# Convolution taps ordered behind the query and key operands, one pass for both key ranges, other tap rates: a two-layer trunk on one Trainium2 core

## The chip, the cores and the metric

The kernel runs on one core of a Trainium2 chip. The metric is the device time of one execution in microseconds; lower is better. The kernel before takes 1058.18 us, the median of 3 runs (1057.49 to 1059.27). One of its executions was also profiled, and every number on where time goes comes from that one.

## The reference

A trunk of two layers over 256 latent tokens (a grid of 4 rows by 64 columns) and 256 context tokens, all in fp32, model width 1024. The part of a layer that matters here:

```python
def conv_branch(p_glu, dw, dw_b, ln_g, ln_b, w_o):
    a, g = jnp.split(p_glu, 2, axis=-1)
    u = a * jax.nn.sigmoid(g)
    u = dwconv1d(u, dw, dw_b)              # depthwise, 31 taps, 512 channels
    u = jax.nn.silu(layernorm(u, ln_g, ln_b))
    return u @ w_o
...
    p = h @ w_in[l]                        # columns: conv | q | k | v | gates
    q = rope_2d(q, pos_row, pos_col)
    k = rope_2d(k, pos_row, pos_col)
    y_conv = conv_branch(p[..., :GLU_END], ...)
    y_attn = merge_heads(neighbourhood_attention(q, k, v, k_c, v_c, na_rpb[l])) @ w_na_out[l]
    x = x + g1 * gated_merge(p[..., QKV_END:], y_conv, y_attn, w_out[l])
```

`neighbourhood_attention` has 8 heads of 64. Each query sees a clamped window of 4 rows by 16 columns, with a bias per relative position, and all 256 context keys, under one softmax. In layer 0 the context tokens run through the same weights (512 columns in all) and attend to each other; in layer 1 only keys and values of the context are needed. A gated MLP with a width-3 convolution follows in each layer.

## The kernel before

**Products.** Activations lie transposed: 128 channels on the partitions, tokens along the free axis. Each fp32 product is three fp32r products on TensorE (PE): high times high (L197), high times low of the activation (L198), low of the weight times high (L199). A weight block of 128x1024 arrives by DMA, ScalarE (ACT) casts its high part (L167), VectorE (DVE) subtracts to get the low part (L168). For some blocks ACT makes both (L216, L217) and a DMA of POOL adds the raw weight. One `group` is 24 products into one PSUM bank.

**Side work.** Generators are stepped once at each slot, which a group calls at its end, and a group of 512 columns also in its middle. The generators are: the taps of the depthwise convolution (`conv_run`), the attention (`Attention.run`, which issues scores, softmax, transposes and values in steps), the modulation products of the next norms on VectorE (L304), and the norms.

**Taps.** The convolution is 4 channel blocks (`cb[0]` to `cb[3]`) by 31 taps per layer, on VectorE. The first of a block is L671, the others L673: `cb = u * w + cb`, over 128x512 elements in layer 0 and 128x256 in layer 1. `rate` says how many taps a slot issues. `conv_tap` orders a tap behind the instruction that the list `after` holds; that list is filled by the attention alone, with the latest softmax minimum (`scores`, L516: adds the bias and takes the extreme of a row) or maximum (`ctx_scores`, L530). This is an order on VectorE's own queue. After the last tap VectorE adds the four blocks (L949 to L951; the first two on POOL in layer 1), and TensorE sums that over the channels for the LayerNorm (L955).

**Queries and keys.** `qk(j)` handles two heads, j = 0 to 3 ("pair j" below): a group for Q and one for K, then the rotary embedding on VectorE (L859 multiply, L860 shuffle, L861 multiply, L864 or L869 add), then a high part by ACT (L881) and a low part by VectorE (L882). K's latent columns are stored twice, in two ranges of 40 columns by 4 rows (128x160), one for each half of the queries; so K takes an ACT and a VectorE pass for each range and, for its context columns, one more of each that reads the PSUM bank directly.

**Attention.** Scores (TensorE, L495) go to four PSUM tiles (`sc` twice, `pt`, `main`); L516 on VectorE, exponential on ACT (L519), reciprocal on VectorE (L521), scaling on ACT (L522), transposes on TensorE (L561), copies of the transposes out of PSUM on ACT (L564), then values (L578). The context's own softmax has L530, L535, L537, L540 and L567 in these places. It is done for two pairs at a time, so twice in layer 0.

The instructions are put in order on each engine by a scheduler from the program's dependencies, its code order and the `issue_after` hints. Where the PSUM banks and buffers go is decided with it.

## Time and profile before

| what | us |
| --- | --- |
| median of 3 runs | 1058.18 |
| profiled execution | 1054.58 |
| its span, first to last instruction | 1052.8 |
| TensorE busy | 1032.4 (98%) |
| VectorE busy | 893.2 (85%) |
| ScalarE busy | 565.6 (54%) |
| 120 taps of 128x512, layer 0 | 89.1 |
| 120 taps of 128x256, layer 1 | 55.7 |
| mean granted TensorE clock, share of full | 0.997 |

TensorE's busy time is nearly the span, so what is left to read is each stretch in which it waits. A row of the waits says which engine and line waited for which, for how long in total, how often and how long at most. A row of a timeline has the start, the length, the engine, the line, the operation, what it writes and reads, and in brackets the idle time ahead of it and what ended that. The lengths of two rows that follow each other can overlap by a little, since the next instruction starts before the one ahead has written its last result.

### The profile page before, as it was taken

The page shows a single profiled execution, that of the slowest core. Times are in us where ns is not written, and L with a number is a line of the kernel's source. Part 1 is how long each engine was busy: PE and PEld are TensorE (multiplying, and loading weights), DVE is VectorE, ACT ScalarE, POOL GpSimd, SP SyncE. Part 2 cuts the span into 40 slices and gives each one's busy share as a digit, 9 for nine tenths or more (in the row PEclk, how much of TensorE's full clock was granted, in tenths as well). Part 3 has the DMA queues.
Part 4 walks back from the last instruction along what each step waited for, and adds up shares of the span by engine and source line. Part 5 has one row for each costly group of instructions (what it writes and reads, how often), then busy time and mean ns, then how long its engine had stood idle before and what let it go on. Part 6 is the DMA issues. An engine that isn't in the chain of part 4 may idle for free.

```text
span 1052.8 us, 17991 instructions
## 1 busy us (share of the span) xinstructions
PE 1032.4 (98%) x6886; PEld 932.9 (89%) x6886; DVE 893.2 (85%) x1608; ACT 565.6 (54%) x921; POOL 43.7 (4%) x59
## 2 busy tenths in 40 slices
PE   9999999999999999999999999999999999999997
PEld 7787788888889988888888889999889999999996
DVE  6568899999998787878788888799899988988883
ACT  4458768545434644444444223545777666766652
POOL 1111110011000000000000000000000000000000
PEclk9999999999999999999999999999999999999998
DMA  9989674888945345454545887556734485666781
GB/s 374 305 221 229 156 181 121 258 255 236 305 146 177 104 140 160 140 164 143 166 145 160 301 289 249 180 189 209 208 123 135 161 292 176 193 201 199 221 283 57
DMA packets 59511, 209.26 MB, mean 199 GB/s; under 512 B 7201, under 2 KB 7457, under 8 KB 59425
## 3 DMA queue, kind: packets, MB, share of 16 engines
q1 hardware_dynamic: 54384, 190.77, 55.3%
q0 software_dynamic: 4752, 17.30, 8.7%
q8 instruction: 54, 0.88, 0.3%
q14 instruction: 33, 0.26, 0.1%
q10 hardware_dynamic: 288, 0.04, 0.0%
HBM read 187.63 MB, written 1.05 MB: 179 GB/s over the span
## 4 chain that ended last, share of the span: by engine, by line
PE 68%; DVE 17%; ACT 5%; DMA 4%; issue 3%; SPq 1%; DVEq 0%; ACTq 0%
PE main L197 20%; PE main L198 20%; PE main L199 20%; DVE cb L673 6%; PE main L736 4%; DVE wlo L168 3%; DMA raw<-in_wall 2%; DVE t L304 2%; DMA own<-in_wada 1%; SPq L728 1%; PE sc L197 1%; PE sc L199 1%; PE sc L198 1%; DVE qk L882 1%; ACT pp L519 1%
## 5 line engine op out<-in xcount | busy, mean ns | idle before, releaser
L197 PE MATMUL main<-h,whi 128*128 128x256 f32 (+1 forms) x1328 | 433.1, 326 | 1.2 <-DVE qk L882 1.2
L198 PE MATMUL main<-h,whi 128*128 128x256 f32 (+1 forms) x1328 | 430.2, 324 | 0.9 <-DVE h L1001 0.7
L199 PE MATMUL main<-h,wlo 128*128 128x256 f32 (+1 forms) x1328 | 429.9, 324 | 1.2 <-DVE wlo L168 1.1
L167 ACT CAST whi<-raw 128x1024 fp32r<-128x1024 f32 (+1 forms) x211 | 218.3, 1039 | 234.8 <-PE main L198 173.6
L168 DVE TENSOR_TENSOR wlo<-raw,whi 128x1024 fp32r<-128x1024 f32 (+1 forms) x211 | 253.6, 1208 | 67.2 <-ACT whi L167 66.4
L197 PEld LDWEIGHTS main<-h,whi 128*128 128x128 f32 x1328 | 252.8, 190 | 22.0 <-issue 1.3
L199 PEld LDWEIGHTS main<-h,wlo 128*128 128x128 f32 x1328 | 252.5, 190 | 18.5 <-DVE wlo L168 1.8
L198 PEld LDWEIGHTS main<-h,whi 128*128 128x128 f32 x1328 | 252.7, 190 | 18.3 <-DVE h L1001 1.0
L304 DVE CUSTOM_DVE_ANT_0 t<-own,sb,par 128x1024 bf16<-128x1024 f32 x120 | 151.8, 1282 | 6.8 <-DMA own<-in_wada 6.8
L673 DVE SCALAR_TENSOR_TENSOR cb<-u,par,cb 128x512 f32<-128x512 f32 (+1 forms) x240 | 144.7, 620 | 2.8
L198 PE MATMUL main<-fl,whi 128*128 128x256 f32 (+1 forms) x396 | 122.8, 310 | 0.0
L197 PE MATMUL main<-fh,whi 128*128 128x256 f32 (+1 forms) x396 | 122.8, 310 | 0.0
L199 PE MATMUL main<-fh,wlo 128*128 128x256 f32 (+1 forms) x396 | 122.5, 310 | 0.0
L197 PEld LDWEIGHTS main<-fh,whi 128*128 128x128 f32 x396 | 75.6, 191 | 3.8 <-ACT fh L1095 0.2
L198 PEld LDWEIGHTS main<-fl,whi 128*128 128x128 f32 x396 | 75.6, 191 | 3.7 <-DVE fl L1096 0.2
L199 PEld LDWEIGHTS main<-fh,wlo 128*128 128x128 f32 x396 | 75.5, 191 | 3.6
L216 ACT CAST whi<-raw 128x1024 fp32r<-128x1024 f32 x33 | 34.6, 1049 | 36.0 <-PE main L198 30.5
L404 ACT ACTIVATE h<-t,mod 128x256 fp32r<-128x256 f32 x56 | 25.2, 503 | 34.8 <-DVE t L403 34.3
L218 POOL DMA_DIRECT2D wlo<-raw x33 | 28.9, 877 | 258.9 <-ACT wlo L217 107.6
L736 PE MATMUL main<-whi,h 128*128 128x512 f32 x128 | 38.5, 386 | 0.2
L1105 ACT ACTIVATE t<-t 128x512 f32<-128x512 f32 x22 | 13.9, 632 | 41.3 <-DVE t L1074 41.3
L217 ACT ACTIVATE wlo<-whi 128x1024 fp32r<-128x1024 f32 x33 | 35.0, 1061 | 0.5
(214 smaller groups left out, 1268.8 us busy)
## 6 DMA issues: line engine op xcount, KB each, us to landing
raw<-in_wall SPq DMA_DIRECT2D x240, 512.0 KB, 4.3
own<-in_wada SPq DMA_DIRECT2D x72, 512.0 KB, 4.7
wlo<-raw POOLq DMA_DIRECT2D x33, 512.0 KB, 5.4
raw<-in_wada SPq DMA_DIRECT2D x16, 512.0 KB, 5.8
bias<-in_bias_t SPq DMA_DIRECT2D x8, 520.0 KB, 5.3
row<-in_wada SPq DMA_DIRECT2D x8, 512.0 KB, 5.1
sb<-in_crow SPq DMA_DIRECT2D x5, 512.0 KB, 4.8
x<-in_xt SPq DMA_DIRECT2D x4, 512.0 KB, 5.1
```

The source lines that it names most:

```text
L167: act.copy(hi[:, c], r[:, c])
L168: dve.tensor_tensor(lo[:, c], r[:, c], hi[:, c].bitcast(F32), ALU.subtract)
L197: pe.matmul(ps, w[0], order(xh), start=start, stop=False)
L198: pe.matmul(ps, w[0], order(xl), start=False, stop=False)
L199: pe.matmul(ps, w[1], order(xh), start=False, stop=stop)
L216: act.copy(hi, r)
L217: act.mul(lo, hi.bitcast(F32), -1.0)
L218: pool.dma_start(lo, r, accum_op=ALU.add)
L304: dve.tensor_tensor_reduce(tmp().bitcast(BF16), r, v, 1.0, pr(l, BADA + n, 1), ALU.mult, ALU.add, mods[l][:, n, s : s + 1])
L404: high = act.activation(hi[:, c], y[:, c], AF.Identity, bias=b)
L673: dve.scalar_tensor_tensor(cb[j], src, w, cb[j], ALU.mult, ALU.add)
L736: mm = pe.matmul(pv[t], h1[n == 1][k][:, c], runs(w[n == 2][:, b]), start=k + n == 0, stop=k == KD - 1 and n == 2)
```

## The change

Line numbers in the changed kernel are 4 higher up to the taps (a tap is L677 there, a block's first L675), the rotary lines are L865 to L875, ACT's and VectorE's passes L884 and L885, the LayerNorm lines L958 to L967.

1. After each Q and each K operand, `after[0]` is set to the last low part of that operand. Taps that are issued from then on stand behind the whole chain on VectorE.
2. K's two latent ranges are written by one ACT copy (L889) and one VectorE subtraction (L890) over 128x2x4x40 elements. The two ranges are one access pattern with one more dimension, made by the helper `steps`. That is 8 ACT and 8 VectorE instructions less over the 8 K operands.
3. Rates: layer 0 starts at 3 taps a slot (before 2), has 1.5 in Q's and K's groups, and 4 after the first pair (before 3). Layer 1 keeps 3.

```diff
+    def steps(a, first, *dims):
+
+        return bass.AP(tensor=a.tensor, offset=a.offset + first, ap=[a.ap[0], *dims])
...
                 conv = conv_run()
-                rate[0] = 3 if last else 2.0
+                rate[0] = 3.0
                 add_side(conv)
 
                 def qk(j):
 
                     att.ahead(j - 2)
+                    if not last:
+                        rate[0] = 1.5
...
                         else:
-                            rv_ = r1[:, LAT].rearrange("p (r c) -> p r c", r=ROWS)
                             to = [([f[:, a, KCTX] for a in range(2)], ctx_)]
-                            for d, c in ((slice(0, KL), slice(GW - TC, GW)), (slice(KX, KN), slice(0, TC))):
-                                to.append(([f[:, a, d].rearrange("p (c r) -> p r c", r=ROWS) for a in range(2)], rv_[:, :, c]))
                         for (hi, lo), src in to:
                             act.activation(hi, src, AF.Identity, scale=sc)
                             end = dve.scalar_tensor_tensor(lo, src, sc, hi.bitcast(F32), ALU.mult, ALU.subtract)
+                        if what:
+                            hi, lo = (steps(f[:, a], 0, (KX, 2), (1, ROWS), (ROWS, TC)) for a in range(2))
+                            src = steps(r1, GW - TC, (TC - GW, 2), (GW, ROWS), (1, TC))
+                            act.copy(hi, src)
+                            end = dve.tensor_tensor(lo, src, hi.bitcast(F32), ALU.subtract)
+                        after[0] = end
                         both.append(f)
                     att.pair(j, *both, bt, end)
+                    rate[0] = 3.0 if last else 4.0
...
                     for j in range(1, 4):
                         glu_groups(j)
                         qk(j)
-                        rate[0] = 3
```

The rows below are instructions in the order in which an engine has them, without times: line, operation, what it writes and reads, the elements, and a count where a row stands for several. Numbers in names tell buffers apart.

VectorE in layer 0 at K of pair 1 (the scores of this pair are what the prediction calls place A). `main_943` and `main_946` are K's PSUM bank. Before:

```order
L859 TENSOR_TENSOR t_1012<-main_943,rope_196 128x256
L860 STREAM_SHUFFLE t_1013<-main_943 128x256
L673 SCALAR_TENSOR_TENSOR cb_0_184<-u_0_197,par,cb_0_184 128x512
L861 TENSOR_TENSOR t_1013<-t_1013,rope_196 128x256
L882 SCALAR_TENSOR_TENSOR qk_1018<-main_943,qk_1018 128x256
L869 TENSOR_TENSOR t_1012<-t_1012,t_1013 128x256
L673 SCALAR_TENSOR_TENSOR cb_0_184<-u_0_197,par,cb_0_184 128x512 x2
L882 SCALAR_TENSOR_TENSOR qk_1018<-t_1012,qk_1018 128x4x40 x2
L673 SCALAR_TENSOR_TENSOR cb_0_184<-u_0_197,par,cb_0_184 128x512 x3
L516 ISA sc_1063,mx_1079<-sc_1063,bias_893 128x2x208
```

The same engine and place in the changed kernel, from the last rotary addition on:

```order
L875 TENSOR_TENSOR t_1014<-t_1014,t_1015 128x256
L885 SCALAR_TENSOR_TENSOR qk_1020<-main_946,qk_1020 128x256
L890 TENSOR_TENSOR qk_1020<-t_1014,qk_1020 128x2x4x40
L677 SCALAR_TENSOR_TENSOR cb_0_184<-u_0_197,par,cb_0_184 128x512
L675 TENSOR_SCALAR cb_1_185<-u_1_198,par 128x512
L677 SCALAR_TENSOR_TENSOR cb_0_184<-u_0_197,par,cb_0_184 128x512
L677 SCALAR_TENSOR_TENSOR cb_1_185<-u_1_198,par,cb_1_185 128x512
L677 SCALAR_TENSOR_TENSOR cb_0_184<-u_0_197,par,cb_0_184 128x512
L677 SCALAR_TENSOR_TENSOR cb_1_185<-u_1_198,par,cb_1_185 128x512
L516 ISA sc_1065,mx_1081<-sc_1065,bias_897 128x2x208
L516 ISA mx_1081 128x1
L677 SCALAR_TENSOR_TENSOR cb_1_185<-u_1_198,par,cb_1_185 128x512
```

Three taps have left the inside of the chain, six stand between it and the first minimum instead of three, and the minima have a tap between them, where before none stood before the second.

VectorE ahead of the second context softmax of layer 0 (place C). Before:

```order
L673 SCALAR_TENSOR_TENSOR cb_2_186<-u_2_199,par,cb_2_186 128x512 x4
L168 TENSOR_TENSOR wlo_2160<-raw_2158,whi_2159 128x1024
L673 SCALAR_TENSOR_TENSOR cb_2_186<-u_2_199,par,cb_2_186 128x512 x5
L596 TENSOR_TENSOR ol_2_194<-po_1902,oh_2_190 128x4x4x16
L530 TENSOR_REDUCE mx_343_1945<-sc_1917 128x2
```

In the changed kernel:

```order
L677 SCALAR_TENSOR_TENSOR cb_2_186<-u_2_199,par,cb_2_186 128x512
L168 TENSOR_TENSOR wlo_2163<-raw_2161,whi_2162 128x1024
L677 SCALAR_TENSOR_TENSOR cb_2_186<-u_2_199,par,cb_2_186 128x512 x9
L959 TENSOR_TENSOR ss_2225<-ss_2225,cb_2_186 128x512
L596 TENSOR_TENSOR ol_2_194<-po_1900,oh_2_190 128x4x4x16
L530 TENSOR_REDUCE mx_343_1943<-sc_1915 128x2
```

Nine taps of one block and the second LayerNorm addition have taken the place of five taps. Behind the low parts of K of pairs 2 and 3 the changed order likewise has 8 taps of one block each, where 5 and 3 stood. On ACT, a cast of the next weights (L167), which stood ahead of the last two scalings (L540) of this softmax, stands behind them and behind a gate's activation (L715).

TensorE and VectorE at the LayerNorm sum of layer 0 (place D), where `ss` is the sum of the blocks, `po` what TensorE makes of it, and `main_2345` the group after it. TensorE in the changed kernel:

```order
L199 MATMUL main_2288<-h_175,wlo_2292 128x512
L964 MATMUL po_2326<-ss_2225,one 128x512
L197 MATMUL main_2345<-h_168,whi_2347 128x512
L198 MATMUL main_2345<-h_176,whi_2347 128x512
L199 MATMUL main_2345<-h_168,wlo_2348 128x512
```

VectorE there:

```order
L304 ISA t_2320,mod_105<-own_2245,sb_2146,par 128x1024
L304 ISA mod_105 128x1
L960 TENSOR_TENSOR ss_2225<-ss_2225,cb_3_187 128x512
L304 ISA t_2322,mod_105<-own_2245,sb_2149,par 128x1024
L304 ISA mod_105 128x1
L168 TENSOR_TENSOR wlo_2348<-raw_2346,whi_2347 128x1024
```

TensorE's L964 stands one group, 24 products, earlier in the program than L955 did, and the low part of the next group's weights (`wlo_2348`) stands behind the sum and a modulation product. From the first L530 of the second context softmax to L960, VectorE has 28 taps, 1 weight split, 5 modulation products (two rows each) and no other LayerNorm addition; before it had 33 taps and a block's first, 3 splits, 6 modulation products and one addition.

In layer 1 K's group of pair 3 gets another PSUM bank: before, the last reader of its bank was VectorE's pass over the context columns of pair 2's K (L882), now it is ACT's exponential of the last score tile of the softmax that runs then (L519). Ahead of that softmax's minima VectorE has a tap before each, and the shuffle and second multiply of the rotary chain behind them. TensorE's instructions are as many as before.

## The prediction

> **What bounds the kernel now.** I read the busy row of the page first, then TensorE's waits, then the groups of VectorE, then the timelines at each wait that the change could touch. The busy row:
>
> ```profile
> PE 1032.4 (98%) x6886; PEld 932.9 (89%) x6886; DVE 893.2 (85%) x1608; ACT 565.6 (54%) x921; POOL 43.7 (4%) x59
> ```
>
> TensorE (PE) has work in 1032.4 of 1052.8 us, and the change leaves its work alone. So VectorE (DVE) and ScalarE (ACT) count only where TensorE waits for them. The waits of TensorE that name an engine the change touches:
>
> ```profile
> PE sc L495 <- ACT pT L567: 1.7, 1, 1.7
> PE main L197 <- DVE qk L882: 1.2, 2, 0.6
> ...
> PE po L955 <- DVE ss L951: 1.0, 1, 1.0
> PE sc L495 <- ACT qk L881: 0.9, 1, 0.9
> PE sc L495 <- DVE qk L882: 0.6, 1, 0.6
> PE pt L561 <- ACT pp L522: 0.3, 1, 0.3
> ```
>
> The columns are the total, the number of waits and the longest, in us. What the view lists besides lies in norms, weight splits and the program's two ends. These six sum to 1.7 + 1.2 + 1.0 + 0.9 + 0.6 + 0.3 = 5.7 us: that is the ceiling, half a per cent of the time. VectorE in the stretches where most of these waits lie (columns: length, then busy time and count of PE, PEld, DVE, ACT, POOL, then clock, DMA share, GB/s):
>
> ```profile
> 90.00:130.00 40.00, 36.29 (x270) 30.01 (x271) 35.87 (x80) 32.32 (x72) 5.97 (x7) 1.00 0.71 168
> 130.00:180.00 50.00, 49.80 (x344) 41.51 (x342) 46.69 (x100) 37.03 (x84) 4.35 (x5) 1.00 0.64 156
> ```
>
> VectorE is busy 35.9 of 40 and 46.7 of 50 us, so a tap that leaves one place there comes back soon after. What the change can win is order, not work. The groups:
>
> ```profile
> L673 DVE SCALAR_TENSOR_TENSOR cb<-u,par,cb 128x512 f32<-128x512 f32 x120 | 89.1, 751 | 1.5
> L673 DVE SCALAR_TENSOR_TENSOR cb<-u,par,cb 128x256 f32<-128x256 f32 x120 | 55.7, 489 | 1.3
> L882 DVE SCALAR_TENSOR_TENSOR qk<-t,qk 128x160 fp32r<-128x160 f32 x16 | 7.8, 531 | 0.3
> ```
>
> **The price of a merged K copy.** Between the two tap rows 256 more elements cost 751 - 489 = 262 ns, so some 489 - 262 = 227 ns of an instruction do not depend on its length. By that estimate one pass over 320 elements takes 227 + 327 = 0.55 us, where two of 160 take 2 x (227 + 164) = 0.78 us (a row below shows two in 0.81). A merged pair saves about 0.25 us of VectorE. No row shows the four-dimensional pattern: at best it is as dense as estimated, at worst it runs at the 531 ns per 160 of the row above and saves nothing. I take 0.2. Eight pairs are 1.6 us of VectorE, but the path gets it only at the first place below. The Trainium skill, page "VectorE: DVE Perf Modes", section "The TRN2 errata — SBUF-src ops pay a fixed extra latency per instruction", speaks against a gain of this size: its table gives 58 cycles per VectorE instruction, thus 0.06 us at 0.96 GHz for a merged pair, and by it the first place gets 0.15 us less; the tap rows show 227 ns, nearer the longer term that the same section measures, and I go by the rows.
>
> **Place A, scores of pair 1, layer 0.** VectorE, then ACT, then PE:
>
> ```profile
> 92.40 0.42 DVE L859 TENSOR_TENSOR t<-main,rope 128x256 f32<-128x256 f32 x1
> ...
> 93.09 0.74 DVE L673 SCALAR_TENSOR_TENSOR cb<-u,par,cb 128x512 f32<-128x512 f32 x1
> 93.74 0.42 DVE L861 TENSOR_TENSOR t<-t,rope 128x256 f32<-128x256 f32 x1
> ...
> 94.74 1.54 DVE L673 SCALAR_TENSOR_TENSOR cb<-u,par,cb 128x512 f32<-128x512 f32 x2
> 96.20 0.81 DVE L882 SCALAR_TENSOR_TENSOR qk<-t,qk 128x160 fp32r<-128x160 f32 x2
> 96.91 2.33 DVE L673 SCALAR_TENSOR_TENSOR cb<-u,par,cb 128x512 f32<-128x512 f32 x3
> 99.16 0.59 DVE L516 CUSTOM_DVE_ANT_0 sc<-sc,bias 128x416 f32<-128x416 f32 x1
> ```
>
> ```profile
> 94.24 1.08 ACT L217 ACTIVATE wlo<-whi 128x1024 fp32r<-128x1024 f32 x1
> 95.20 0.79 ACT L881 ACTIVATE qk<-t 128x160 fp32r<-128x160 f32 x2
> ...
> 100.44 0.60 ACT L519 ACTIVATE pp<-sc,mx 128x416 f32<-128x416 f32 x1
> ```
>
> ```profile
> 96.04 0.44 PE L495 MATMUL sc<-qk,qk 64*128 64x416 f32 x2 [0.87 <-ACT qk L881]
> 97.07 0.62 PE L495 MATMUL sc<-qk,qk 64*128 64x416 f32 x4 [0.58 <-DVE qk L882]
> ```
>
> Three taps stand inside the K chain: they hold VectorE for 93.74 - 93.09 = 0.65 and 96.20 - 94.74 = 1.46 us. In the new order all three leave. K's sum is then ready near 93.8, and ACT, which copies transposes until L217 starts at 94.24, makes K's two high parts by about 95.0 (its L217 now stands behind). The merged low part ends near 95.5, not 97.0. TensorE is through with its group at 95.0 and waits next to nothing: **-1.4 us** (0.87 + 0.58).
>
> Most of that comes back. Six taps instead of three now stand ahead of the first minimum (L516), alternating between two blocks. Two taps in a row on one block start 0.78 apart (2.33 / 3); a tap before another operation holds VectorE 0.65. Six at 0.65 are 3.9 us, so the first minimum starts at 95.5 + 3.9 = 99.4 (before: 99.16), and two more taps stand between the minima. The second minimum starts at 99.4 + 0.51 + 0.65 = 100.6, its exponential at 101.2 instead of 100.44. The transposes wait for the last scaling (0.3 us before, ACT L522); it ends 0.3 to 0.9 us later than before. So A nets between -1.0 (ACT absorbs it) and +0.9; I take **+0.4**. The transposes' copies (L564), which stood behind an L217 with 0.3 us of waiting, no longer do: **-0.3**.
>
> **Place B, scores of pair 2.** DVE, ACT and PE:
>
> ```profile
> 124.85 0.43 DVE L869 TENSOR_TENSOR t<-t,t 128x256 f32<-128x256 f32 x1
> ...
> 125.32 0.81 ACT L881 ACTIVATE qk<-t 128x160 fp32r<-128x160 f32 x2 [1.58 <-DVE t L869]
> ...
> 127.02 1.06 ACT L217 ACTIVATE wlo<-whi 128x1024 fp32r<-128x1024 f32 x1
> 127.98 1.05 ACT L567 COPY pT<-sc 128x512 f32<-128x512 f32 x2
> ...
> 128.60 1.28 PE L495 MATMUL sc<-qk,qk 64*128 64x416 f32 x6 [1.69 <-ACT pT L567]
> ```
>
> The context copies (L567) free the score banks. ACT runs them after L881, L216 and L217, and L881 waited 1.58 us for VectorE's K chain, in which two taps (2 x 0.65) stood ahead of L869. Without these and with the merged copy the whole ACT train moves up 1.6 to 2.0 us, and the wait of 1.69 goes: **-1.7**, or -0.9 if L216's weight buffer comes free late; a shorter train (0.2) adds up to -0.2. I take **-1.9**. Running sum at 130 us: 0.4 - 0.3 - 1.9 = -1.8.
>
> **Place C, second context softmax.** Here VectorE sets the pace, as the window row shows, and TensorE's lead is handed back:
>
> ```profile
> 166.29 3.90 DVE L673 SCALAR_TENSOR_TENSOR cb<-u,par,cb 128x512 f32<-128x512 f32 x5
> ...
> 170.75 1.28 DVE L530 TENSOR_REDUCE mx<-sc 128x2 f32<-128x512 f32 x2
> ...
> 177.49 1.06 ACT L167 CAST whi<-raw 128x1024 fp32r<-128x1024 f32 x1
> 178.42 0.93 ACT L540 ACTIVATE pp<-pp,ri 128x256 f32<-128x256 f32 x2
> ```
>
> VectorE starts this stretch some 0.4 late (A). Between the two context softmaxes the new order has two taps fewer (-1.3), two passes fewer by the merging (-0.4) and one LayerNorm sum more (0.69 by the row at D). And it sets 8, 8 and 9 taps in a row on one block where 5, 3 and 5 stood: 12 more starts at 0.78 instead of 0.65, +1.6. Together 0.4 - 1.3 - 0.4 + 0.7 + 1.6 = +1.0 us, of which VectorE's idle time in the window (50.00 - 46.69 = 3.3 us, spent waiting for exponentials) takes up part. I take +0.3 of it, so L530 at 171.05, between -1.0 and +1.0. ACT's cast L167, which stood ahead of the last two scalings (178.42 - 177.49 = 0.93), now stands behind them. The last scaling ends 0.3 - 0.93 = -0.6 from where it did. TensorE cannot pass it, so of the -1.8 only **-0.6** is left: 1.2 us returned. Bounds: -1.8 if VectorE gets there 1.0 early, +0.1 if 1.0 late.
>
> **Place D, the LayerNorm sum of layer 0.**
>
> ```profile
> 209.73 0.38 PE L199 MATMUL main<-h,wlo 128*128 128x512 f32 x1
> 209.94 0.38 PE L197 MATMUL main<-h,whi 128*128 128x512 f32 x1
> ...
> 212.27 0.69 DVE L951 TENSOR_TENSOR ss<-ss,cb 128x512 f32<-128x512 f32 x1
> ...
> 213.02 1.12 PE L955 MATMUL po<-ss,one 128*128 128x512 f32 x2 [0.97 <-DVE ss L951]
> ```
>
> Products start 0.216 apart. Four taps a slot finish the convolution sooner, and TensorE's L955 stands 24 products earlier, 24 x 0.216 = 5.2 us: without its wait it would have started at 212.0, now at 212.0 - 5.2 - 0.6 = 206.2. VectorE has from L530 to L951 six taps of 0.65, two weight splits and one modulation product of 1.2 each and one LayerNorm sum fewer, -8.1, and with the 0.3 of C its L951 ends at 212.96 - 7.8 = 205.2. The 0.97 goes. But the next group's low weights now stand behind that sum and one modulation product: ready at 205.2 + 1.2 + 1.2 = 207.6, when TensorE wants them at 206.2 + 4 x 0.216 = 207.1. D gives -1.0 + 0.5 = **-0.5**, between -1.0 and +1.0 (one more modulation product ahead costs 1.2).
>
> **Layer 1.** Two products wait for a bank that K's low part (L882) read:
>
> ```profile
> 761.65 0.45 PE L197 MATMUL main<-h,whi 128*128 128x512 f32 x1 [0.55 <-DVE qk L882]
> ...
> 777.14 0.38 PE L197 MATMUL main<-h,whi 128*128 128x256 f32 x1 [0.63 <-DVE qk L882]
> ...
> 761.62 0.61 ACT L519 ACTIVATE pp<-main,mx 128x416 f32<-128x416 f32 x1
> ```
>
> The new order gives the first product another bank, freed by the exponential of the last score map, which ended at 762.2 before and gets two to three taps of 0.4 us ahead of it, less the two rope rows that now stand behind it: +0.3. The second wait should go: -0.6; the chains ahead are shorter: -0.2. **-0.5**, between -1.4 and +1.5.
>
> Sum: -0.6 - 0.5 - 0.5 = **-1.6 us**. The profiled execution took 1054.58 us (span 1052.8 and 1.8 around it), so it should take 1053.0. The median of the runs, 1058.18, lies 3.6 higher; I keep that distance: **1056.6 us**.
>
> **Rivals.** (1) Nothing is given back: A -1.4, B -1.9, D -1.0, layer 1 -1.2, together -5.5, or 1052.7. For it: each of these waits names exactly the chains that shrink. Against it: VectorE's load at C. (2) Slower: the bulk of taps decides. One mechanism, the taps between a chain and the minima of its scores. If each of the four softmaxes of layer 0 and two in layer 1 comes out one tap late past what ACT absorbs (0.65 and 0.4 us), the price is 4 x 0.65 + 2 x 0.4 = 3.4 us, of which the -1.4 at A pays less than half since C resets the rest: about +2.5, or 1060.7. It decides once the second exponential starts later than 101.2. Six taps for three speaks for it; the alternating blocks (0.65, not 0.78) against. (3) The change does not do what it says: all 248 taps remain, so TensorE's lead is fully handed back at C, and at D the late weights cost what the sum's wait did: 0, or 1058.2.
>
> **How the numbers follow.** The forecast has 0.40, with an own range of 1055 to 1058; rival 1 has 0.24, rival 3 0.16 and rival 2 0.20. A measurement of this kernel tells 0.2%, 2.1 us, from no change, so 1056.1 is the bound for faster, and 0.17 of the forecast lies below it. Faster: 0.17 + 0.24 + 0.01 of rival 3 = 0.42. Slower: 0.17 of rival 2 and 0.02 of rival 3 = 0.19. The same: 0.39. The range takes in most of rivals 1 and 2: 1053 to 1060.3.
>
> **What would show it.** Right: K's low parts end within 0.5 us of TensorE's arrival at A; no wait for ACT L567; a wait of 1 to 2 us at the transposes of pair 1 and before the second context softmax; none at the LayerNorm sum; layer 1's wait at 761 names ACT. Wrong: minima that start over 0.7 us later than 99.4 (rival 2); L530 before 170 (rival 1); an L890 longer than 0.8 us, which undoes the merging.

## The result: slower by half a per cent

The changed kernel takes 1063.13 us, the median of 6 runs (1061.73 to 1064.05). Beside it the kernel before takes 1057.84 us (6 runs, 1055.06 to 1059.76). The ratio is 1.0050, 95% interval 1.0034 to 1.0067: slower, where 1056.6 us and no change to a small gain were forecast. Timed again in a later session, beside experiments, the ratio was 1.0081 (1.0062 to 1.0100). The two intervals only just overlap, so the size of the loss may differ between sessions, and each experiment below is compared with the kernel before of its own session.

The busy row and the granted clock by slices of the changed kernel's page:

```profile
PE 1034.0 (97%) x6886; PEld 933.4 (88%) x6886; DVE 898.1 (85%) x1600; ACT 565.4 (53%) x913; POOL 43.7 (4%) x59
...
PEclk9999998999999999999999999999999999999998
```

The span grew from 1052.8 to 1061.4 us, by 8.6 (the profiled execution of before was among its fastest, so this is more than the 5.3 of the medians). TensorE's busy time grew by 1.6 us with the same number of products, and the clock shows an 8 in the seventh slice, 159 to 186 us. The rest is waiting. TensorE's waits in the changed kernel (total, times, longest, in us):

```profile
PE main L197 <- ACT pp L519: 2.0, 1, 2.0
...
PE main L197 <- DVE qk L885: 1.6, 1, 1.6
PE main L197 <- ACT h L1009: 1.5, 1, 1.5
PE po L578 <- DVE ol L596: 1.4, 1, 1.4
PE pt L561 <- ACT pp L540: 1.2, 1, 1.2
PE sc L561 <- ACT pp L540: 1.1, 2, 0.7
PE sc L561 <- ACT pp L522: 1.1, 2, 0.7
...
PE sc L495 <- ACT qk L889: 0.8, 1, 0.8
...
PE pt L561 <- ACT pp L522: 0.7, 1, 0.7
PE sc L561 <- ACT pp L535: 0.6, 1, 0.6
...
PE sc L495 <- DVE qk L890: 0.4, 1, 0.4
```

The waits for the context copies (L567) and for the LayerNorm sum are gone, as forecast. Those for softmax results (L519, L522, L535, L540) have come or grown, 6.7 us together. Setting the start of the same TensorE product in both traces side by side gives the lag of the changed kernel; a negative change is a gain:

| stretch | lag at its end, us | change | forecast |
| --- | --- | --- | --- |
| to 111 us, scores and transposes of pair 1 (A) | +1.0 | +1.0 | +0.1 |
| to 129 us, scores of pair 2 (B) | -0.8 | -1.8 | -1.9 |
| to 187 us, second context softmax (C) | +5.3 | +6.2 | +1.2 |
| to 214 us, LayerNorm sum (D) | +4.1 | -1.2 | -0.5 |
| to 301 us, next norm | +5.3 | +1.2 | none |
| 750 us to the end, layer 1 | +8.5 | +3.1 | -0.5 |

Place C is the largest. VectorE there, in the changed kernel:

```profile
167.31 7.05 DVE L677 SCALAR_TENSOR_TENSOR cb<-u,par,cb 128x512 f32<-128x512 f32 x9
174.40 0.69 DVE L959 TENSOR_TENSOR ss<-ss,cb 128x512 f32<-128x512 f32 x1
...
175.34 1.28 DVE L530 TENSOR_REDUCE mx<-sc 128x2 f32<-128x512 f32 x2
```

L530 starts at 175.34, where 171.05 was forecast and 170.75 stood before. TensorE behind it:

```profile
181.84 0.37 PE L561 MATMUL pt<-ident,pp 64*128 64x64 f32 x1 [1.18 <-ACT pp L540]
...
183.54 1.97 PE L578 MATMUL po<-pT,V 128*64 128x256 f32 x8
185.30 1.07 PE L587 MATMUL po<-pT,VW 128*64 128x64 f32 x16
186.30 0.74 PE L197 MATMUL main<-h,whi 128*128 128x512 f32 x1
```

The same products in the kernel before:

```profile
179.74 1.08 PE L578 MATMUL po<-pT,V 128*64 128x256 f32 x8
180.65 0.63 PE L587 MATMUL po<-pT,VW 128*64 128x64 f32 x16
181.22 0.48 PE L197 MATMUL main<-h,whi 128*128 128x512 f32 x1
```

The L197 after this place starts 186.30 - 181.22 = 5.1 us later, and the values (L578) themselves take 1.97 instead of 1.08 us. The windows of 1 us show why (columns: length, busy time and count of PE, PEld, DVE, ACT, POOL, then granted clock, DMA share, GB/s):

```profile
177.00:178.00 1.00, 0.27 (x3) 0.02 (x1) 0.77 (x2) 1.00 (x5) 0.00 (x0) 1.00 0.89 324
178.00:179.00 1.00, 0.42 (x5) 0.28 (x7) 0.19 (x2) 1.00 (x4) 0.00 (x0) 1.00 0.30 119
179.00:180.00 1.00, 0.57 (x9) 0.29 (x7) 1.00 (x2) 1.00 (x5) 0.00 (x0) 1.00 0.00 0
180.00:181.00 1.00, 0.58 (x6) 0.40 (x6) 0.96 (x3) 1.00 (x6) 0.00 (x0) 0.51 0.00 0
...
186.00:187.00 1.00, 1.00 (x10) 0.81 (x7) 0.96 (x3) 0.72 (x2) 0.00 (x0) 0.58 0.00 0
187.00:188.00 1.00, 1.00 (x7) 0.87 (x6) 0.96 (x2) 0.00 (x0) 0.00 (x0) 1.00 0.86 303
```

After three windows in which TensorE was busy for 0.27 to 0.57, its clock is at half from 180.0 until 186.8 (a mean of 0.58 in the window from 186 means 0.84 us at half). L578 and L587 alone lose 0.89 + 0.44 = 1.3 us by that. The prediction had nothing of the kind. The Trainium skill, page "TensorE: Matmul & The Clock Gate", section "Part 1: The HAM clock gate (the "warmup" mystery)", states that the array falls to half clock after an activity window of about 3.4 us that was idle; the trace agrees on the half and roughly on the window, though TensorE was not idle here but busy for 0.27 to 0.57 of each microsecond.

### The profile page after: what moved, and what is told of

Read it like the earlier page. It is cut to its first block, busy times and chain, and to the rows that moved or that the text cites. A ratio compares the mean times of both kernels' runs of the same rounds, so it can differ in the third digit from the quotient of the medians.

```text
span 1061.4 us, 17964 instructions
## 1 busy us (share of the span) xinstructions
PE 1034.0 (97%) x6886; PEld 933.4 (88%) x6886; DVE 898.1 (85%) x1600; ACT 565.4 (53%) x913; POOL 43.7 (4%) x59
## 4 chain that ended last, share of the span: by engine, by line
PE 78%; DVE 12%; ACT 4%; DMA 3%; issue 2%; SPq 1%; DVEq 0%; ACTq 0%
PE main L197 22%; PE main L198 22%; PE main L199 22%; PE main L740 4%; DVE cb L677 3%; DVE wlo L168 3%; DMA raw<-in_wall 2%; SPq L732 1%; PE sc L197 1%; PE sc L199 1%; PE sc L198 1%; ACT pp L519 1%; PE po L230 1%; PE po L578 1%; ACT whi L167 1%
## 5 line engine op out<-in xcount | busy, mean ns | idle before, releaser
L197 PE MATMUL main<-h,whi 128*128 128x256 f32 (+1 forms) x1328 | 433.2, 327 | 5.0 <-ACT pp L519 2.0
L167 ACT CAST whi<-raw 128x1024 fp32r<-128x1024 f32 (+1 forms) x211 | 218.2, 1038 | 233.1 <-PE main L198 174.1
L197 PEld LDWEIGHTS main<-h,whi 128*128 128x128 f32 x1328 | 252.9, 190 | 25.7 <-ACT pp L519 2.2
L677 DVE SCALAR_TENSOR_TENSOR cb<-u,par,cb 128x512 f32<-128x512 f32 (+1 forms) x240 | 146.8, 616 | 4.5
L197 PE MATMUL main<-fh,whi 128*128 128x256 f32 (+1 forms) x396 | 122.8, 310 | 0.0
L197 PEld LDWEIGHTS main<-fh,whi 128*128 128x128 f32 x396 | 75.6, 191 | 3.7 <-ACT fh L1104 0.2
```

The source lines that it names most:

```text
L167: act.copy(hi[:, c], r[:, c])
L197: pe.matmul(ps, w[0], order(xh), start=start, stop=False)
L677: dve.scalar_tensor_tensor(cb[j], src, w, cb[j], ALU.mult, ALU.add)
```

## Experiments

**Theory Q** (the queueing): taps inside a Q or K chain were nearly free, since they filled waits of that chain; pushed behind it, they leave VectorE waiting, come back later as a lump, and make the softmaxes late. **Theory R** (the rates): more taps in the slots before the context softmaxes make these late. **Theory I**: it is idle time of VectorE as such that costs, however it arises, above all in chains without taps. **Theory B** (bulk): it is the taps that stand in a row between a chain and its minima. I and B are two readings of Q. The merged pass is the third part of the change. All kernels were timed in 5 rounds.

**One part alone.** `q_only` is the kernel before with part 1 of the change, `r_only` with part 3, `m_only` with part 2; `no_r` is the change with the old rates.

```diff
 q_only, on the kernel before
+                        after[0] = end
                         both.append(f)
 r_only, on the kernel before
-                rate[0] = 3 if last else 2.0
+                rate[0] = 3.0
...
+                    if not last:
+                        rate[0] = 1.5
...
+                    rate[0] = 3.0 if last else 4.0
...
-                        rate[0] = 3
 m_only, on the kernel before
-                            for d, c in ((slice(0, KL), slice(GW - TC, GW)), (slice(KX, KN), slice(0, TC))):
-                                to.append(...)
+                        if what:
+                            act.copy(hi, src)
+                            end = dve.tensor_tensor(lo, src, hi.bitcast(F32), ALU.subtract)
```

> The kernel before with the queueing alone (after[0] = end after each Q and K operand); rates 2/3 and K's two separate passes as before. Theory Q (queueing): without taps inside the chains VectorE idles there for ACT (0.25 + 1.14 + 0.48 + 0.87 us in the changed kernel between the two context softmaxes) and the taps run in a row on one block at 0.78 instead of 0.65 us; the second context softmax's first L530 then starts at 173 to 175 us (before 170.75, changed 175.34), TensorE waits there for ACT's scalings, and the kernel is 3 to 5 us slower. Theory R (rates): 90 taps stand ahead of that L530 as before, it starts near 171, and the kernel is between 2 us faster and 1 us slower.

> The kernel before with the new rates alone (3 at the start, 1.5 in Q's and K's groups, 4 after the first pair, layer 0); no queueing, K's two separate passes. Theory R: 96 taps instead of 90 stand ahead of the second context softmax, 6 x 0.65 to 0.78 = 3.9 to 4.7 us, so its first L530 starts at 174 to 175.5 us, TensorE waits there and falls to half its clock for some us, and the kernel is 3 to 5 us slower. Theory Q: VectorE's waits for ACT shrink with the taps in the chains and take up the six taps; L530 starts by 172 and the kernel is within 1 us of the one before.

> The kernel before with K's two ranges in one ACT copy and one VectorE subtraction alone. In the changed kernel that subtraction took 0.76 to 0.84 us where the two passes took 0.81 to 0.86, so both theories expect nothing: within 1 us of the kernel before, L530 of the second context softmax at 170.2 to 171 us.

> The changed kernel with the old rates: queueing and the merged K pass, 2 taps a slot and then 3. Theory Q: 3 to 5 us slower than before, L530 of the second context softmax at 173 us or later. Theory R: L530 near 171 us with 90 taps ahead of it, no half clock there, and between 2 us faster and 1 us slower than before.

Measured, beside 1056.62 us for the kernel before:

| kernel | median, us | ratio, 95% interval | second L530, us |
| --- | --- | --- | --- |
| `q_only` | 1061.85 | 1.0050 (1.0031 to 1.0070) | 173.96* |
| `r_only` | 1055.52 | 0.9983 (0.9967 to 0.9999) | 171.38 |
| `m_only` | 1058.62 | 1.0011 (0.9994 to 1.0029) | 172.26* |
| `no_r` | 1063.92 | 1.0070 (1.0049 to 1.0090) | 175.70* |

The last column is the start of the first L530 of the second context softmax in the one execution that was profiled. A star says that TensorE's clock was at half for 3.4 or 6.9 us between 97 and 111 us of that execution, ahead of this place. Such a stretch can make everything behind it late, so a starred time does not tell by itself what the edit did there.

Queueing alone costs what the whole change costs. The rates alone gain a little, at the edge of what the interval tells. The merged pass shows no difference that its interval tells; its median is 2.0 us higher, where at most 1 was expected. Theory R falls: with six more taps ahead of it, L530 of `r_only` starts at 171.38, not at 174 or later, and the kernel is not slower.

**Where queueing is done.** `no_q` is the change without it, `q_layer0` and `q_layer1` with it in one layer, and `q_sum` queues the taps behind the rotary addition instead of the low part, so that they may fill the wait for ACT's high part.

```diff
 no_q
-                        after[0] = end
 q_layer0 (q_layer1 with "if last")
-                        after[0] = end
+                        if not last:
+                            after[0] = end
 q_sum
-                            dve.tensor_tensor(r1[:, LAT], r1[:, LAT], r2[:, LAT], ALU.add)
+                            after[0] = dve.tensor_tensor(r1[:, LAT], r1[:, LAT], r2[:, LAT], ALU.add)
...
-                        after[0] = end
```

> The changed kernel without its queueing line (new rates and merged K pass kept). Queueing alone cost 0.5%, rates alone won 0.17%, the merged pass alone moved nothing that its interval tells (0.1%, -0.06 to 0.29). If the three parts add up this is within 1.5 us of the kernel before, and the second context softmax's first L530 is at 171 to 172.5 us. If the parts only hurt together, it is 2 us or more away.

> The changed kernel with the queueing in layer 0 only. Theory 0: the loss lies in layer 0 (softmaxes of pair 1 and of the contexts, with the half clock there): 3 to 5 us slower than before, and as the kernel before in layer 1. Theory 1: it lies in layer 1, where the first K group waits for an exponential: within 1.5 us of before. From the profiled executions alone, 5.4 us are lost up to 323 us and 3 more in layer 1; so I lean to about 60% of the loss, 3 us.

> The changed kernel with the queueing in layer 1 only. Theory 0: within 1 us of before. Theory 1: 3 to 5 us slower. By the profiled executions about 2 to 3 us slower, with the wait of TensorE L197 for ACT L519 at some 760 us still there (2.0 us in the changed kernel, 2.7 with queueing alone).

> The changed kernel, but the taps are queued behind the rotary sum of each Q and K operand instead of behind its last low part, so taps may stand between the sum and the low parts, while VectorE waits for ACT's high parts. Theory I (idle VectorE): the loss comes from VectorE idling in the chains for ACT (2.7 us between the context softmaxes); here it nearly vanishes, L530 of the second context softmax starts by 172 us, and the kernel is from 2 us faster to 1 us slower than before. Theory B (bulk): the loss comes from the taps in bulk ahead of and between the minima, which stay: 3 to 5 us slower, L530 at 174 us or later.

Measured, beside 1055.95 us:

| kernel | median, us | ratio, 95% interval | second L530, us |
| --- | --- | --- | --- |
| `no_q` | 1055.88 | 1.0002 (0.9989 to 1.0014) | 175.85* |
| `q_layer0` | 1061.29 | 1.0048 (1.0034 to 1.0063) | 176.11 |
| `q_layer1` | 1060.59 | 1.0040 (1.0027 to 1.0053) | 172.74 |
| `q_sum` | 1060.80 | 1.0040 (1.0025 to 1.0055) | 173.20 |

Without queueing the loss is gone. Yet L530 of `no_q` starts at 175.85, as late as in the changed kernel, where 171 to 172.5 was expected. Its profiled execution is the slowest of its twelve (1060.85 us), and in it TensorE waited 2.4 us for a K operand at pair 1 and then ran at half clock from 98.0 to 104.9:

```profile
98.00:99.00 1.00, 0.66 (x4) 0.65 (x6) 1.00 (x3) 0.97 (x2) 0.04 (x1) 0.52 0.89 311
...
104.00:105.00 1.00, 1.00 (x4) 0.82 (x3) 1.00 (x3) 0.86 (x2) 0.00 (x0) 0.57 0.71 172
```

So this trace can't stand for the kernel's usual execution, and a late L530 alone is no proof of a loss by queueing.

Queueing in either layer loses nearly as much as the change lost in its first session, more than was expected of either (3 us, and 2 to 3). The two sum to 0.88%, near the 0.81% of the change in its later session but not its 0.50%, so I can't say how much each layer has in the whole. `q_sum` is at most a little better. VectorE is idle for only 8.7 us from its first tap to the second L530, less than in `r_only` (9.4), and the loss is still there: its 3 to 5 us are what theory B expected, not what theory I did. L530 at 173.20 lies between the two.

**Free chains without queueing.** `early_74` and `early_90` take the kernel before and lower layer 0's rate to 1 tap a slot from K's group until the scores are issued, with 3 and 4 (4 and 5) elsewhere. The chains are short of taps, but no tap is ordered behind them.

```diff
 early_74 (early_90 with 4 for 3 and 5 for 4)
+            if not self.l:
+                self.rate[0] = 4.0
...
-                rate[0] = 3 if last else 2.0
+                rate[0] = 3 if last else 3.0
...
+                        if not last:
+                            rate[0] = (3.0, 1.0)[what]
...
+                    if not last:
+                        rate[0] = 1.0
```

> The kernel before with other rates in layer 0 alone, no queueing and no merging: 3 taps a slot, 3 in the Q group, 1 from the K group until the scores of the pair are issued, then 4. The chains then hold about as few taps as in the changed kernel (one or two in K's), and the minima follow K's last low part with no tap or one between; 74 taps stand ahead of the second context softmax. Theory B (bulk): what costs is the taps that queueing puts between chain and minima; with them out of the way from both places this gains what the prediction hoped for, 1 to 4 us faster than before, and loses some at the LayerNorm sum of layer 0, which has 50 taps still to come instead of 34. Theory I (idle VectorE in chains without taps): no faster than before, 0 to 4 us slower.

> As the kernel with 74 taps ahead of the second context softmax, but 4 taps a slot at the start and in the Q groups, 1 from the K group to the scores, then 5: 88 taps ahead of that softmax. Theory B: 2 to 4 us faster than before, and no wait at the LayerNorm sum. Theory I: 0 to 4 us slower than before.

Measured, beside 1056.34 us: `early_74` 1062.24, ratio 1.0054 (1.0037 to 1.0070), `early_90` 1064.39, ratio 1.0071 (1.0044 to 1.0097). The row of VectorE's first minimum in `early_74` (the bracket has VectorE's idle time ahead of it; this kernel's L518 and L497 are the L516 and L495 of the kernel before), then two of TensorE's waits in `early_90`:

```profile
77.70 0.60 DVE L518 CUSTOM_DVE_ANT_0 sc<-sc,bias 128x416 f32<-128x416 f32 x1 [5.66 <-PE sc L497]
```

```profile
PE po L960 <- DVE ss L956: 2.7, 1, 2.7
PE main L199 <- DVE wlo L168: 2.6, 3, 1.2
```

VectorE idles 5.66 us at one place, the taps that it could have done are done later, and now the LayerNorm sum and weight splits are late. Theory B alone fails here, since it expected a gain; theory I has the sign right, but the losses of 5.90 and 8.05 us lie above its 0 to 4. These kernels also put more taps into the other slots and finish the taps later, so they don't show idle time by itself. And more idle time is not what `q_only` shows: from its first tap to the second L530, at the same 90 taps, `q_only` is idle for 13.4 us and the kernel before for 13.4 too (with 3.4 us at half clock in `q_only`). What is slower there is told below.

**The half clock.** `warm` adds products of 128x128 ahead of the transposes of the second context softmax, 28 calls of two passes each, some 7 us in all where 28 x 0.112 = 3.1 us were reckoned with, so that TensorE stays busy; nobody reads their results.

```diff
                 for i, pp in enumerate(pps[n]):
+                    if what == CTX and its[0][0] == 2:
+                        for _ in range(7):
+                            pe.matmul(outs[0][:, i, 0:2].rearrange("p s q -> p (s q)"), ident, ident, start=True, stop=True)
```

> The changed kernel with 7 products of 128x128 more ahead of each of the four sets of transposes of the second context softmax (28 in all, 0.112 us each, into the bank that the transposes then overwrite; they compute nothing that is used). They run while TensorE waits there for ACT's scalings (4.5 us in the changed kernel's profile, ahead of 6.5 us at half clock). Theory C (clock): the half clock costs time of its own; without it this is 1.5 to 3 us faster than the changed kernel, so 2 to 4 us slower than before, with a mean clock of 0.995 or more and no half clock from 175 to 200 us. If only the wait costs: as the changed kernel, 5 us slower than before, or more.

Measured: 1065.19 beside 1056.34 us, 1.0080 (1.0056 to 1.0104). The clock stays at full through this place, but the added products took longer than the 2.9 us of waits ahead of the transposes in the changed kernel, so the total says nothing of what the half clock cost. `warm2` has fewer, beside the changed kernel itself (`after_again`, no edit) on one chip:

```diff
 warm2, on warm
-                        for _ in range(7):
+                        for _ in range((3, 2, 1, 4)[2 * n + i]):
```

> The changed kernel as it is, timed beside the next two, since it has not stood beside experiments yet. Expected 1.005 of the kernel before, between 1.003 and 1.007, with the clock at half for some 6 us before the values of the second context softmax of layer 0.

> The changed kernel with 10 products of 128x128 that nobody reads (two passes each, some 2.6 us in all) placed only where TensorE waited for ScalarE's scalings ahead of the transposes of the second context softmax of layer 0: 3, 2, 1 and 4 of them, less than the waits there. If the half clock that the trace shows there costs time of its own, it goes or shortens and this kernel takes 1 to 2.5 us less than the changed kernel (about 0.999 of it). If VectorE's late maxima alone set the end of this place, so that TensorE would wait for them anyway, the clock is at full and the time stays within 0.5 us of the changed kernel. The products themselves cost nothing by either theory, since they lie in waits.

Measured, beside 1056.42 us: `after_again` 1065.72, 1.0081 (1.0062 to 1.0100); `warm2` 1065.05, 1.0074 (1.0057 to 1.0092). The windows of `warm2`:

```profile
180.00:181.00 1.00, 1.00 (x13) 0.81 (x13) 1.00 (x3) 1.00 (x4) 0.00 (x0) 1.00 0.69 279
181.00:182.00 1.00, 0.95 (x11) 0.67 (x10) 0.96 (x2) 1.00 (x6) 0.00 (x0) 1.00 0.00 0
182.00:183.00 1.00, 0.18 (x4) 0.05 (x2) 1.00 (x5) 1.00 (x5) 0.00 (x0) 0.86 0.00 0
183.00:184.00 1.00, 0.97 (x9) 0.67 (x9) 0.96 (x2) 1.00 (x4) 0.00 (x0) 0.50 0.00 0
```

In this execution the half clock came all the same, from 182.7 to 189.6. But it was the slowest of the six runs of `warm2` and had the lowest mean clock (0.993). In the mean of the runs the clock was 0.9952, against 0.9928 for `after_again`, and still the mean time is only 0.3 us lower. Either the half clock costs little of its own here, or the added products cost what it gave back; these runs can't tell which, since none has this place at full clock and nothing else changed.

A bound comes from the runs themselves. Over 87 runs of the kernel before, 0.001 less mean granted clock goes with 1.14 us more time (a fitted slope). By that slope the clock has these parts in the losses (means of the runs):

| kernel | loss, us | mean clock lost | part of the clock, us |
| --- | --- | --- | --- |
| `after_again` | 8.4 | 0.0023 | 2.6 |
| `q_layer0` | 5.3 | 0.0025 | 2.8 |
| `q_layer1` | 4.3 | 0.0003 | 0.3 |
| `q_only` | 4.6 | 0.0004 | 0.4 |
| `no_r` | 6.7 | 0.0007 | 0.8 |

So `q_only`, `no_r` and `q_layer1` lose their time with hardly any lower clock, while of what `q_layer0` loses about half goes with the clock. This is an estimate: the slope is a correlation, and waits of TensorE can come together with a lower clock.

**Which chain.** `q_k` queues taps behind K's chain alone, `q_q` behind Q's alone.

```diff
 q_k (q_q with "if not what")
-                        after[0] = end
+                        if what:
+                            after[0] = end
```

> The change, with taps queued behind K's chain alone and not behind Q's. If what costs is that dependent rows of a chain without taps leave VectorE waiting, half of the chains are free again and the loss shrinks to about half: 1.0025 of the kernel before, between 1.001 and 1.004. If it is the taps that stand between K's chain and its minima, the loss is as in the changed kernel, 1.005. If it is Q's chain alone, none is left: 1.000.

> The change, with taps queued behind Q's chain alone, the complement of the run with K's chain alone (1.0085, where the changed kernel had 1.0081). If the queue behind K carries the whole loss, this kernel comes out as the change without any queueing, 1.000, between 0.9985 and 1.0015, and the first L530 of the second context softmax is back at 172 or less. If every chain that is kept free costs its own part and the two overlap at the same places, it loses too, 1.003 or more.

Measured: `q_k` 1066.72 beside 1056.42 us, 1.0085 (1.0066 to 1.0104), as much as the whole change there; `q_q` 1059.46 beside 1055.61 us, 1.0029 (1.0016 to 1.0041). Half the chains free did not mean half the loss. K's queue alone loses as much as both, which is what was expected if the taps between K's chain and its minima decide (theory B); and yet Q's alone is not free either. The softmax maxima of `q_k`:

```profile
176.50 1.28 DVE L530 TENSOR_REDUCE mx<-sc 128x2 f32<-128x512 f32 x2
```

They are later than the changed kernel's 175.34, and those of `q_q`, at 175.17, are not back at 172. But both executions had a stretch at half clock ahead of this place (106.8 to 110.2, and 97.5 to 104.4), so these two times say nothing of Q's or K's taps.

## Why the prediction was wrong

**The step that failed** is "VectorE starts this stretch some 0.4 late (A)" with its sum "0.4 - 1.3 - 0.4 + 0.7 + 1.6 = +1.0 us" and "so L530 at 171.05". It let VectorE's idle time take up 0.7 of the 1.0 us, and it had no term for rows of a chain that follow each other without a tap. From the first row of the first context softmax to that of the second (109.36 to 170.75 before, 110.66 to 175.34 in the changed kernel, both at full clock up to there) the terms came out so:

| term, us | forecast | measured |
| --- | --- | --- |
| start of the stretch | +0.4 | +1.30 |
| taps, two fewer and more in a row | -1.3 + 1.6 | -0.53 |
| low parts | -0.4 | +0.16 |
| LayerNorm sum and other rows | +0.7 | +0.46 |
| rotary rows | none | +0.90 |
| idle time | -0.7 | +2.30 |
| L530 | +0.3 | +4.59 |

The taps themselves cost less than was forecast. The idle time, which was 3.45 us and was to shrink, grew to 5.75, and 3.0 of that stands ahead of rows of the chains, where none stood before. The start is late by 1.30, with 44 taps done by then instead of 36, and the rotary rows take 0.90 more.

At place A the forecast took it that a tap that leaves a chain gives back the 0.65 us for which it held VectorE there. What it really gives back is read at the first pair, which the prediction passed over. VectorE in `r_only`, which has the new rates and no queueing (a tap is L677, a low part L888):

```profile
61.83 0.42 DVE L865 TENSOR_TENSOR t<-main,rope 128x256 f32<-128x256 f32 x1
...
70.95 1.06 DVE L888 SCALAR_TENSOR_TENSOR qk<-t,qk 128x160 fp32r<-128x160 f32 x2
71.88 7.03 DVE L677 SCALAR_TENSOR_TENSOR cb<-u,par,cb 128x512 f32<-128x512 f32 x9
78.83 0.59 DVE L516 CUSTOM_DVE_ANT_0 sc<-sc,bias 128x416 f32<-128x416 f32 x1
```

and in the changed kernel:

```profile
61.25 0.42 DVE L865 TENSOR_TENSOR t<-main,rope 128x256 f32<-128x256 f32 x1 [0.86 <-PE main L199]
...
63.51 0.42 DVE L885 SCALAR_TENSOR_TENSOR qk<-t,qk 128x256 fp32r<-128x256 f32 x1 [0.54 <-ACT qk L884]
...
68.66 0.42 DVE L885 SCALAR_TENSOR_TENSOR qk<-main,qk 128x256 fp32r<-128x256 f32 x1 [0.50 <-ACT qk L884]
...
70.16 1.02 DVE L890 TENSOR_TENSOR qk<-t,qk 128x320 fp32r<-128x320 f32 x1 [1.08 <-ACT qk L889]
71.08 8.60 DVE L677 SCALAR_TENSOR_TENSOR cb<-u,par,cb 128x512 f32<-128x512 f32 x11
79.59 0.59 DVE L516 CUSTOM_DVE_ANT_0 sc<-sc,bias 128x416 f32<-128x416 f32 x1
```

The tap behind K's low part starts 71.88 - 71.08 = 0.80 us earlier. For that VectorE waited 0.86 us for TensorE ahead of Q's chain and 0.54 + 0.50 + 1.08 = 2.12 us inside the two chains, and at its first minimum, itself 0.76 us later, it has done 17 taps where `r_only` has done 22. The five are owed, and both kernels stand at 96 taps by the second L530, at 171.38 and 175.34. Up to there the clock is full in both traces, so they can be compared. VectorE's rows from the first tap to that point, sorted by what they are (time from one start to the next, idle time apart):

| us | `r_only` | changed kernel |
| --- | --- | --- |
| 96 taps; of these followed by a tap | 66.2; 50 | 67.3; 61 |
| 32 rotary rows | 10.9 | 12.6 |
| low parts (20 rows; 16) | 7.2 | 7.4 |
| all other rows | 19.4 | 18.7 |
| idle | 9.4 | 11.1 |
| sum | 113.2 | 117.1 |

The 3.9 us between them are +1.1 for taps (0.72 each before another tap, 0.66 before something else), +1.6 for rotary rows (0.39 instead of 0.34 each, where dependent rows follow each other without a tap), +1.7 of idle time (+7.0 ahead of rows of the chains, 0.86 of it for TensorE at the first one, and -5.3 elsewhere), +0.2 for low parts and -0.7 for the rest. The prediction had a term of the first kind alone. The kernel before and `q_only`, at 90 taps each, differ by +1.6 for taps and +1.4 for rotary rows out of 3.2, without more idle time. The sorting shows where VectorE's time went in these executions; no run changed one of these parts alone.

**Place A: +0.4 - 0.3 forecast, +1.0 measured.** VectorE at A:

```profile
95.66 0.76 DVE L890 TENSOR_TENSOR qk<-t,qk 128x320 fp32r<-128x320 f32 x1 [0.82 <-ACT qk L889]
...
97.44 2.74 DVE L677 SCALAR_TENSOR_TENSOR cb<-u,par,cb 128x512 f32<-128x512 f32 x4
100.09 0.60 DVE L516 CUSTOM_DVE_ANT_0 sc<-sc,bias 128x416 f32<-128x416 f32 x1
```

The low part starts at 95.66, where the forecast had it end at 95.5: with no tap to cover it, the chain waits 0.82 us for ACT. TensorE still waits 0.8 and 0.4 us for the operands, so the gain of 1.4 that was to come from these waits did not come, and the sign "within 0.5 us of TensorE's arrival" failed. The first minimum starts at 100.09, 0.69 later than the 99.4 of the forecast, just short of the "over 0.7" that it named for rival 2, and the transposes then wait 1.1 + 0.7 us for ACT L522, as the sign "1 to 2 us" had it. That the minima come late behind six taps was foreseen; that a chain standing alone waits for ACT was not.

**Place B: right.** No wait for L567, and -1.8 us measured for -1.9. **Place D: right in kind.** The wait for the sum is gone, -1.2 us for -0.5, but TensorE came there 5.3 us late, so the forecast's own times were not put to the test. At C TensorE handed back its whole lead of 0.9 us and 5.3 us more.

**Layer 1: -0.5 forecast, +3.1 measured.** The bank's new reader was named rightly, its time wrongly. VectorE, ACT and TensorE there:

```profile
766.79 0.58 DVE L516 CUSTOM_DVE_ANT_0 main<-main,bias 128x416 f32<-128x416 f32 x1
```

```profile
767.24 1.17 ACT L522 ACTIVATE pp<-pp,ri 128x416 f32<-128x416 f32 x2
768.31 0.60 ACT L519 ACTIVATE pp<-main,mx 128x416 f32<-128x416 f32 x1
```

```profile
769.05 0.48 PE L197 MATMUL main<-h,whi 128*128 128x512 f32 x1 [1.98 <-ACT pp L519]
```

The exponential starts at 768.31 instead of 761.62, 6.7 later, with a lag of 5.4 on arrival: it is 1.3 us late, where +0.3 stood. The last minimum has a tap ahead of it, and on ACT two scalings stand between the third exponential and this one, where none stood. The old reader of that bank would not have been sooner: its pass (L885) starts at 769.43 in this order. The later waits in the list, 1.6 for L885 and 1.4 for L596, stand behind minima and taps in the same way, but no run tested them. The 1.5 for L1009 (the next norm) was not looked at further: `r_only`, which is not slower, has it too.

**The merged pass.** The groups of VectorE:

```profile
L890 DVE TENSOR_TENSOR qk<-t,qk 128x320 fp32r<-128x320 f32 x8 | 7.3, 918 | 6.2 <-ACT qk L889 6.2
```

Eight passes keep VectorE busy for 7.3 us where sixteen kept it for 7.8: 0.06 us saved a pair, not the 0.2 taken. The 0.06 that the Trainium skill's page "VectorE: DVE Perf Modes" gave (section "The TRN2 errata — SBUF-src ops pay a fixed extra latency per instruction") is what was measured; the estimate from the tap rows, which I preferred, was three times too high. One pass takes 918 ns in the mean, over the 0.8 us that the prediction named as a sign that undoes the merging; but two passes took 531 ns each, so a little is saved all the same. The row also shows where the queueing went: 6.2 us of idle time ahead of the eight, 0.3 ahead of the sixteen.

**The rivals.** Rival 2 named the right kind, lateness of the minima behind a bulk of taps, at 1060.7, and its own condition was met: the second exponential at A starts at 101.96, later than 101.2. Its price is 2.4 us too low. Lump and empty chain are two ends of one thing, since a tap pushed out of a chain stands behind it. `q_sum` and `q_k` came out as the lump would have it; `early_74` and `early_90`, with no lump ahead of the minima, lose too. The rows add that the chain gains only a fraction of what the lump costs. Rival 1 is excluded at the maxima (L530 at 175.34, not before 170), rival 3 by the interval. The range, 1053.0 to 1060.3, took its upper end from these prices and so missed by 2.8 us.

**What stays open.** `no_q` and `q_only` show that the queueing costs the time. They don't show how the loss divides into lump, empty chain and half clock; nor is it known why the losses of the two chains don't add up, and why the loss is 0.5% in one session and 0.8% in another.

The best kernel found is `r_only`, the new rates without queueing, 0.17% faster than before (0.01 to 0.33%). Of its 2.0 us in the means 1.2 go with a higher clock by the slope above, and `no_q`, which has the same rates and the merged pass, shows no gain.

## What to carry to other kernels

On an engine that is nearly always busy, an independent instruction between two dependent ones can be close to free, and taking it out to shorten a chain buys a fraction of its length (here 0.8 us for five taps, which take 0.66 to 0.72 us each when they come back). Before such a reorder, read what the chain waits for once it stands alone: the other engine's pass (ACT's high part here), and the latency of dependent rows. Count how much independent work is done by each deadline, not only what stands ahead of it there. And before one trace is set against another, compare their clocks up to the place in question: `no_q`, which is not slower, has as late an L530 as the changed kernel.

## What the hardware showed that was not expected

- VectorE's price of an instruction depends on what follows it: a tap takes 0.72 us when another tap is next (0.78 on the same block) and 0.66 otherwise, and rotary rows take 0.39 us in the mean in a chain by themselves and 0.34 with taps between.
- In the changed kernel TensorE's clock fell to half after 3 us at a busy share of 0.27 to 0.57, and it stayed there for 6.8 us (180.0 to 186.8), although TensorE was fully busy again after 182. In `warm2` it fell at 182.7, after windows of 1.00, 0.95 and 0.18, and came back at 189.6. So the busy share of the last 3 us in a profile does not tell by itself when the clock falls.
- Ahead of the program's end, the stretches at half clock in these traces lasted either 3.4 or 6.8 to 6.9 us. A wait of TensorE alone does not tell whether one comes: after waits of 1.3 to 2.4 us for K's operand at pair 1 the clock fell within some 2 us in the traces of `no_q`, `m_only`, `early_74` and `q_q`, but not after 1.5 us in that of `r_only`, nor after 1.9 us in that of `no_r`.
